# Pair sums and splits regrouped around the gating pair of a one-layer decoder block

## The chip, the core and the metric

The kernel runs on one core of a Trainium2 chip. The metric is the device time of one execution in microseconds. TensorE (PE in the profile) multiplies, VectorE (DVE) and ScalarE (ACT) do elementwise work, GpSimd (POOL) does little here, and SyncE (SP) issues nearly all loads.

## The reference

One layer over 256 tokens of width 2048, all in float32:

```python
h = rms_norm(x, norm_mix_pre)
proj = h @ w_in                                  # columns of A, B, C and the merge gates
y_a = conformer_conv(a_in, ...)                  # GLU, causal conv, layer norm, swish, projection
y_b = chunked_spatial_gating(b_in, ...)          # gelu, spatial mix by chunks, projection
y_c = native_sparse_attention(q, kv, nsa_g, ...) # three attention branches, projection
g_a, g_b, g_c = split(sigmoid(merge_g), 3)
mixed = (g_a * y_a + g_b * y_b + g_c * y_c) @ w_o
x = x + rms_norm(mixed, norm_mix_post)
h = rms_norm(x, norm_ffn_pre)
u = causal_depthwise_conv(h @ w_up, ...)
x = x + rms_norm((silu(u_g) * u_v) @ w_down, norm_ffn_post)
```

## The kernel before, in words

**Products of split numbers.** Every float32 matrix operand is split into a rounded high part and the rest: ScalarE copies the high part (`whi`, or `whiwraw` where it goes through `weights`), VectorE subtracts it from the raw weights (`wlo`, `wlowraw`). A product is three matmuls: high by high, high by low, low by high. Weights come as tiles of 128 x 1024 into `wraw`, a ring of five buffers; the high parts and the rests have a ring of four each. A load can start when its buffer's last reader is done, a split when TensorE has read the buffer it writes.

**Sevens.** Three products, the last gating pair (column blocks 2 and 3 of branch C's merge gates), the first half of `w_o` and both halves of `w_down`, run in a scheme of seven products for a 2 x 2 block of 128 x 512 tiles (`class Seven`). It needs sums of pairs of k-tiles, on the activations' side (`sums4`, `input_sums`) and on the weights' side (in `seven`, on VectorE and ScalarE: parts named b, a, t and 4). A call works through plain k-tiles of 12 matmuls each and quads of 21; `in_sevens` uses 10 plain k-tiles (k = 6 to 15) and 3 quads (k = 0 to 5). Four banks (`pga`, `poa`) hold the main results, four others (`pgb`, `pob`) the side results that `combine` adds up.

**The order of the work.** The stages are: input projections with the attention spread between them; `branch` for B, A and C, each of which multiplies gate columns (`pg`), takes the tanh of the gates (`mg`), multiplies a branch's projection (`py`) and adds the gated product into `mac`. Branch C is called for blocks 0 and 1 only. Then comes the gating pair (`in_sevens` into `pga` and `pgb`), its results `gates` (VectorE adds, ScalarE tanh), the projections of C for blocks 2 and 3 (`pyc`, `pyd`), the output pair (`po2`, in `poa` and `pob`), the rest of `w_o`, and the feed-forward part with `w_up` and `w_down` (`Pair(0)` in `pd0a` and `pd0b`, `Pair(1)` in `pd1a` and `pd1b`).

**Who decides the order.** Each engine works through its instructions in the order in which they stand. A scheduler sets that order by priority; `fixed` chains an instruction behind the last `fixed` one of its engine (`seq`), `order_of` sets where these chains begin, `in_line` chains matmuls, and `issue_after` puts one instruction behind another. Background generators (`bg`) are advanced by `pump` and `until`. `mix_gen(cb)` is one of them: for block `cb` it transposes `mac` on TensorE (`pm`), splits it into `mh` (ScalarE) and `ml` (VectorE), and for the first three pairs of k-tiles copies the transposed blocks (`ma`, ScalarE) and calls `sums4`, whose adds go to `spm` and `sqm` and whose results are split into `sm`. `sm` is read by the quads of the output pair.

**The last norm.** `fin` holds the down projection's result `res` (columns 0 to 4095), a row of weights `gain` (from 4096) and two scratch areas of 1536 columns for the quads (from 5120 and from 6656). `result` adds a bank to a part of `res` and sums its squares on ScalarE; `weigh` multiplies a part by `gain`, on VectorE. The first half's four parts are weighed during the second pass over `w_down`; then the other half of the row is loaded over `gain`.

Of the kernel before, what the change touches and what calls it, by code (L numbers as in the profile page):

```python
# [25 lines left out]
R = mybir.dt.float32r  # L26
AF = mybir.ActivationFunctionType
# [30 lines left out]
def block(ctx: ExitStack, tc: tile.TileContext, x, xf, fp, cst, rows, sgw, w1, w2, wf_a, wt_bv, wf_bu, wf_c,  # L58
# [197 lines left out]
    def s8(shape, dt, name):  # L256
        return P1.tile(shape, dt, tag="s8", bufs=4, name=name)
# [631 lines left out]
    def fixed(eng, op, *args, **kw):  # L889

        with ExitStack() as order:
            order.enter_context(tc.high_priority())
            for ins in seq.get(eng, ()):
                order.enter_context(tc.issue_after(ins))
            seq[eng] = [op(*args, **kw).ins]  # L895

    def order_of(last):
        seq[V] = seq[S] = list(last)
# [90 lines left out]
    mac = s16(P0, [128, 2, D], F32, "mac")  # L989
    mix = {}  # L990

    def branch(bi, act_of):

        for cb in range(2 if bi == 2 else 4):
            pg = [PS.tile([128, 512], F32, tag="acc", name=f"pg{bi}{cb}{t}") for t in range(2)]
            for q in range(4):
                hs = granule(wt_g[(bi * 4 + cb) * 4 + q])
                for k in range(4 * q, 4 * q + 4):
                    hi, lo = hs[(k % 4) // 2]
                    c = slice((k % 2) * 512, (k % 2) * 512 + 512)  # L1000
                    for t in range(2):
                        ts = slice(t * 128, t * 128 + 128)
                        mm_t(pg[t], hT[:, k, 0, ts], hT[:, k, 1, ts], hi[:, c], lo[:, c], k == 0, k == KT - 1)
                if q < 3:
                    pump(BUDGET)
            tgs = {}
            for t in range(2):
                for a in range(2):
                    tgs[t, a] = q1(f"mg{bi}{cb}{t}{a}")
                    with tc.high_priority(offset=int(PR)):  # L1010
                        S.activation(tgs[t, a], pg[t][:, a * 256:a * 256 + 256], AF.Tanh, scale=rh[:, t:t + 1])
            marks.add("gates")
            pump(BUDGET)
            py = [PS.tile([128, 512], F32, tag="acc", name=f"py{bi}{cb}{t}") for t in range(2)]
            for q in range(2):
                hs = granule(wt_p[(bi * 4 + cb) * 2 + q])
                if cb == 0 and q == 0:
                    until("BAC"[bi])
                    if bi == 2:
                        mix["h"] = s16(P1, [128, KT, T], R, "mh")  # L1020
                        mix["l"] = s16(P1, [128, KT, T], R, "ml")
                act = act_of()
                for k in range(4 * q, 4 * q + 4):
                    hi, lo = hs[(k % 4) // 2]
                    c = slice((k % 2) * 512, (k % 2) * 512 + 512)
                    for t in range(2):
                        ts = slice(t * 128, t * 128 + 128)
                        pe_last[0] = mm_t(py[t], act[:, k, 0, ts], act[:, k, 1, ts], hi[:, c], lo[:, c], k == 0, k == 7)
                if q == 0:
                    pump(BUDGET)  # L1030
            for t in range(2):
                for a in range(2):
                    cc = slice(cb * 512 + a * 256, cb * 512 + a * 256 + 256)
                    y = mac[:, t, cc] if bi == 0 else tgs[t, a]
                    with tc.high_priority(offset=int(PR)):
                        V.scalar_tensor_tensor(y, tgs[t, a], 1.0, py[t][:, a * 256:a * 256 + 256], op0=ALU.add,
                                               op1=ALU.mult)
                        if bi:
                            V.tensor_add(mac[:, t, cc], mac[:, t, cc], y)
            if bi == 2:  # L1040
                bg.append(mix_gen(cb))
            pump(BUDGET)

    def mix_gen(cb):

        for j in range(2 * cb, 2 * cb + 2):
            pt = bank([128, 2, T], f"pm{j}")
            ks = slice(2 * j, 2 * j + 2)
            for i in range(2):
                for t in range(2):  # L1050
                    PE.transpose(pt[:, i, t * 128:t * 128 + 128], mac[:, t, (2 * j + i) * 128:(2 * j + i) * 128 + 128],
                                 ident)
            S.activation(mix["h"][:, ks], pt, AF.Copy, scale=0.5)
            V.scalar_tensor_tensor(mix["l"][:, ks], pt, 0.5, mix["h"][:, ks].bitcast(F32), op0=ALU.mult,
                                   op1=ALU.subtract)
            yield 500
            if j < NG:
                a = [q1(f"ma{j}{i}") for i in range(2)]
                for i in range(2):
                    S.activation(a[i], pt[:, i], AF.Copy, scale=0.5)  # L1060
                if j % 2 == 0:
                    mix[j // 2] = s8([128, 2, 2, 4, 128], R, f"sm{j}")
                sums4(a[0], a[1], mix[j // 2][:, j % 2], f"m{j}")
                yield 1500

    branch(0, lambda: Bt_box["t"])
    branch(1, lambda: At)
# [17 lines left out]
    def acts_h(j):  # L1085
        s1, s2, s4, s3 = parts(sh[:, j], range(4))
        return s4, hx(2 * j + 1, H1), hx(2 * j, H1), s1, s3, s2, hx(2 * j + 1, H2)

    order_of(())
    in_sevens(pr, wt_gp, wt_gq, hx, acts_h, tt, "g")  # L1090
    for n in range(2):
        for t in range(2):
            fixed(V, V.tensor_add, gates[:, t, n], pr.c[t][n], gates[:, t, n])
            fixed(S, S.activation, gates[:, t, n], gates[:, t, n], AF.Tanh, scale=rh[:, t:t + 1])
    pump(1e6)
    Ct = Ct_box["t"]
    for n in range(2):
        cb = 2 + n
        py = [bank([128, 512], f"pyc{t}") if n == 0 else PS.tile([128, 512], F32, tag="acc", name=f"pyd{t}")
              for t in range(2)]  # L1100
        for k in range(8):
            if k % 2 == 0:
                hi, lo = weights(wt_p[(8 + cb) * 2 + k // 4][:, k % 4 * 512:k % 4 * 512 + 1024])
            c = slice(k % 2 * 512, k % 2 * 512 + 512)
            for t in range(2):
                ts = (H1, H2)[t]
                in_line(mm_t, py[t], Ct[:, k, 0, ts], Ct[:, k, 1, ts], hi[:, c], lo[:, c], k == 0, k == 7)
        for t in range(2):
            cc = slice(cb * 512, cb * 512 + 512)
            with tc.high_priority(offset=int(PR)):  # L1110
                V.scalar_tensor_tensor(gates[:, t, n], gates[:, t, n], 1.0, py[t], op0=ALU.add, op1=ALU.mult)
                V.tensor_add(mac[:, t, cc], mac[:, t, cc], gates[:, t, n])
        bg.append(mix_gen(cb))
        pump(1e6)
# [277 lines left out]
    P2c = ctx.enter_context(tc.tile_pool(name="p2c", bufs=1))  # L1392
    fin = P0.tile([128, 8192], F32, tag="hT", name="fin")
    res = fin[:, 0:4096].rearrange("p (t n) -> p t n", t=2)
    gain = fin[:, 4096:5120]
    turn = [0]

    def scratch():
        turn[0] ^= 1
        return fin[:, 5120 + 1536 * turn[0]:6656 + 1536 * turn[0]]  # L1400

    ss3 = PZ.tile([128, 2, 8], F32, name="ss3")
    G.memset(ss3, 0.0)
    nc.sync.dma_start(gain, row(2048, 1024))


    order_of(())
# [1 line left out]
    class Pair(Seven):  # L1409
# [40 lines left out]
                                   accum_out=ss3[:, t, col + 1:col + 2])  # L1450

        def weigh(self, t, n, do=loose):
            do(V, V.tensor_mul, self.at(t, n), self.at(t, n), gain[:, n * 512:n * 512 + 512])

    NP, NQ, KEEP = len(PLAIN), len(PAIRS), 6

# [14 lines left out]
    for j in range(NQ):  # L1471
        while i < (3, 5, 7, 9, 10, 12, 14, 15, 17, 18)[j]:
            second.plain(i)
            if i == 2:
                for t in range(2):
                    for n in range(2):
                        first.result(t, n, fixed)
            elif 3 <= i < 7:
                first.weigh((i - 3) // 2, (i - 3) % 2, fixed)
            elif i == 9:  # L1480
                nc.sync.dma_start(gain, row(3072, 1024))
            i += 1
        second.quad(j)
        if j == 5:
            back = s16(P0, [128, 2, D], F32, "back")
            for t in range(2):
                nc.sync.dma_start(back[:, t], spill[:, t])
        for x in range(0 if j < NQ - 5 else 1 if j < NQ - 1 else KEEP - 4):
            k = NP - KEEP + len(kept)
            into = None  # L1490
            if j < NQ - 1:
                kt = P2.tile([128, 11, T], R, tag=("gh", "gl")[j % 2], bufs=4, name=f"kept{k}")
                into = kt[:, 0:8].rearrange("p (a b) c -> p a (b c)", a=2)
            kept.append((PLAIN[k], weights(wt_dn[1, k], into)))
    assert i == NP - KEEP and len(kept) == KEEP
    second.combine()
    for t in range(2):
        for n in range(2):
            c = slice(n * 512, n * 512 + 512)
# [141 lines left out]
```

## Time and profile before

| | us |
|---|---|
| median of 3 runs | 1584.13 |
| lowest and highest run | 1583.61, 1585.96 |
| profiled execution | 1585.73 |
| its span | 1584.0 |
| mean granted clock of TensorE | 0.996 of full |
| TensorE busy | 1565.5 |
| VectorE busy | 1275.7 |
| ScalarE busy | 907.1 |
| loaded from memory | 301.23 MB, 193 GB/s over the span |

Lines such as `687.65 0.39 PE L198 MATMUL py<-whi,Ct 128*128 128x512 f32 x1` are rows of the timeline: start in us from the span's start, duration, engine, source line, operation, what is written and what is read, shape, how many. Matmuls overlap, so their pace is read from start to start and not from the duration. A bracket at the end gives the idle time of the engine before the row and the instruction that ended it. In the list of waits a row reads: engine, what it wants to do and its line, who released it, us in total, how often, the longest.

### The profile page before, as it was taken

The page shows a single profiled execution, that of the slowest core. Times are in us where ns is not written, and L with a number is a line of the kernel's source. Part 1 is how long each engine was busy: PE and PEld are TensorE (multiplying, and loading weights), DVE is VectorE, ACT ScalarE, POOL GpSimd, SP SyncE. Part 2 cuts the span into 40 slices and gives each one's busy share as a digit, 9 for nine tenths or more (in the row PEclk, how much of TensorE's full clock was granted, in tenths as well). Part 3 has the DMA queues.
Part 4 walks back from the last instruction along what each step waited for, and adds up shares of the span by engine and source line. Part 5 has one row for each costly group of instructions (what it writes and reads, how often), then busy time and mean ns, then how long its engine had stood idle before and what let it go on. Part 6 is the DMA issues. An engine that isn't in the chain of part 4 may idle for free.

```text
span 1584.0 us, 22431 instructions
## 1 busy us (share of the span) xinstructions
PE 1565.5 (99%) x8155; PEld 1326.1 (84%) x8155; DVE 1275.7 (81%) x2192; ACT 907.1 (57%) x1462; POOL 17.8 (1%) x46
## 2 busy tenths in 40 slices
PE   9999999999999999999999999999999999999997
PEld 7888899888888787777888888888888888888876
DVE  7899999867866655477787988888777777899997
ACT  7544544447637675655465656565555555556563
POOL 1000020000000000000000000000000000000000
PEclk9999999999999999999999999999999999999999
DMA  9555566666765544445784666666656666766672
GB/s 375 186 190 184 187 179 208 195 187 186 243 194 155 160 146 153 139 160 188 245 273 145 210 192 188 193 188 189 187 188 192 191 190 190 232 205 209 213 268 78
DMA packets 85440, 307.95 MB, mean 194 GB/s; under 512 B 9808, under 2 KB 10832, under 8 KB 84304
## 3 DMA queue, kind: packets, MB, share of 16 engines
q1 hardware_dynamic: 83952, 301.91, 60.0%
q0 software_dynamic: 944, 4.19, 0.7%
q8 instruction: 64, 1.05, 0.3%
q10 hardware_dynamic: 432, 0.41, 0.1%
q14 instruction: 48, 0.39, 0.1%
HBM read 301.23 MB, written 4.19 MB: 193 GB/s over the span
## 4 chain that ended last, share of the span: by engine, by line
PE 50%; DVE 2%; DMA 1%; issue 0%; ACT 0%; DVEq 0%; ACTq 0%
PE ps L176 20%; PE ps L183 10%; PE pd0b L930 5%; PE pd1a L930 4%; PE poa L930 2%; PE pd0a L930 2%; PE po L196 1%; PE po L198 1%; PE po L197 1%; PE pd1b L930 1%; DMA wraw<-in_wt_dn_dram 1%; PE pob L930 1%; DVE wlowraw L895 0%; DVE fin L895 0%; PE pu L1239 0%
## 5 line engine op out<-in xcount | busy, mean ns | idle before, releaser
L148 DVE TENSOR_TENSOR wlo<-wraw,whi 128x1024 fp32r<-128x1024 f32 x400 | 486.7, 1219 | 116.0 <-ACT whi L147 109.5
L147 ACT ACTIVATE whi<-wraw 128x1024 fp32r<-128x1024 f32 x400 | 419.0, 1053 | 187.3 <-PE pg L198 78.4
L176 PE MATMUL ps<-h2T,whi 128*128 128x512 f32 x1360 | 325.0, 391 | 0.0
L176 PEld LDWEIGHTS ps<-h2T,whi 128*128 128x128 f32 x1360 | 249.8, 188 | 48.2
L183 PEld LDWEIGHTS ps<-h2T,wlo 128*128 128x128 f32 x1360 | 174.5, 191 | 6.7
L183 PE MATMUL ps<-h2T,wlo 128*128 128x256 f32 x1360 | 176.6, 283 | 0.0
L176 PE MATMUL ps<-hT,whi 128*128 128x512 f32 x640 | 157.4, 392 | 0.0
L218 ACT ACTIVATE t<-ps 128x256 f32<-128x256 f32 x125 | 47.6, 382 | 187.1 <-PE ps L176 186.6
L176 PEld LDWEIGHTS ps<-hT,whi 128*128 128x128 f32 x640 | 116.0, 188 | 21.3
L198 PE MATMUL pg<-whi,hT 128*128 128x512 f32 x320 | 125.8, 393 | 0.0
L197 PE MATMUL pg<-wlo,hT 128*128 128x512 f32 x320 | 125.8, 393 | 0.0
L196 PE MATMUL pg<-whi,hT 128*128 128x512 f32 x320 | 122.2, 393 | 0.0
L895 DVE TENSOR_TENSOR wlowraw<-wraw,whiwraw 128x1024 fp32r<-128x1024 f32 x72 | 87.0, 1224 | 33.6 <-ACT whiwraw L895 32.5
L219 DVE TENSOR_TENSOR t<-ps,t 128x256 f32<-128x256 f32 x125 | 52.7, 422 | 70.3 <-ACT t L218 69.8
L479 DVE SCALAR_TENSOR_TENSOR cv<-hb,fps,cv 128x256 f32<-128x256 f32 x240 | 105.0, 478 | 0.2 <-ACT cv L475 0.2
L895 ACT ACTIVATE whiwraw<-wraw 128x1024 fp32r<-128x1024 f32 x72 | 75.4, 1056 | 43.6 <-PE pyc L198 9.0
L183 PEld LDWEIGHTS ps<-hT,wlo 128*128 128x128 f32 x640 | 84.7, 190 | 4.7
L183 PE MATMUL ps<-hT,wlo 128*128 128x256 f32 x640 | 86.8, 283 | 0.0
L197 PEld LDWEIGHTS pg<-wlo,hT 128*128 128x128 f32 x320 | 60.1, 188 | 13.7 <-issue 1.1
L198 PEld LDWEIGHTS pg<-whi,hT 128*128 128x128 f32 x320 | 60.1, 188 | 12.7 <-issue 0.7
L196 PEld LDWEIGHTS pg<-whi,hT 128*128 128x128 f32 x320 | 59.8, 188 | 12.4 <-issue 0.3
L1372 ACT ACTIVATE fa<-fs,fps 128x256 f32<-128x256 f32 x88 | 52.5, 597 | 1.2 <-DVE fs L221 0.9
(1258 smaller groups left out, 2659.3 us busy)
## 6 DMA issues: line engine op xcount, KB each, us to landing
wraw<-in_wf_up_dram SPq DMA_DIRECT2D x176, 512.0 KB, 4.3
wraw<-in_wt_g_dram SPq DMA_DIRECT2D x80, 512.0 KB, 4.1
wraw<-in_wt_p_dram SPq DMA_DIRECT2D x48, 512.0 KB, 4.2
wraw<-in_wt_dn_dram SPq DMA_DIRECT2D x48, 512.0 KB, 4.5
wraw<-in_wf_a_dram SPq DMA_DIRECT2D x32, 512.0 KB, 4.1
wraw<-in_wt_dq_dram SPq DMA_DIRECT2D x20, 512.0 KB, 4.8
qa<-in_wt_dq_dram SPq DMA_DIRECT2D x20, 512.0 KB, 4.2
wraw<-in_wf_bu_dram SPq DMA_DIRECT2D x16, 512.0 KB, 4.4
```

The costliest lines, as they stand in the source:

```text
L147: S.activation(hi[:, :n], raw[:, :n], AF.Copy)
L148: V.tensor_sub(lo[:, :n], raw[:, :n], hi[:, :n].bitcast(F32))
L176: ins = PE.matmul(ps[:, :, ts], lhsT=ws[k // 8][0][:, c:c + 128], rhs=mov[:, k, :, ts], start=(k == 0 and not t), stop=(k == n - 1), skip_ ...
L183: ins = PE.matmul(ps[:, 1, ts], lhsT=ws[k // 8][1][:, c:c + 128], rhs=mov[:, k, 0, ts], start=False, stop=False, skip_group_check=True).ins
L196: PE.matmul(ps, lhsT=xh, rhs=hi, start=first, stop=False)
L197: PE.matmul(ps, lhsT=xh, rhs=lo, start=False, stop=False)
L198: return PE.matmul(ps, lhsT=xl, rhs=hi, start=False, stop=last).ins
L219: V.tensor_add(t1 if rb is not None else dst, ps[:, 0], t1)
L479: V.scalar_tensor_tensor(ca[:, j], hb[:, j, k:k + T], w(j, k), ca[:, j], op0=ALU.mult, op1=ALU.add)
L895: seq[eng] = [op(*args, **kw).ins]
L930: ins = PE.matmul(bank, lhsT=a[x], rhs=w[y], start=first and j == 0, stop=last and j == 2).ins
L1372: S.activation(a, s, AF.Identity, bias=fps[:, C_FB + f:C_FB + f + 1], scale=w[2])
```

## The change

It has three parts.

1. `mix_gen` no longer calls `sums4`; it leaves its `ma` copies in `mix["a", j]`. The three calls stand behind the last of the gating pair's result adds (`issue_after(seq[V][0])`). All background work that is left is pumped before the gating pair instead of after it, and ScalarE's chain of the gating pair begins behind the last tanh of branch C's gates (`gated`).
2. The splits for three of the eight weight tiles of `pyc` and `pyd` are put into the two engines' chains ahead of the gating pair's results: two ahead of all of them, the third ahead of those of block 3.
3. `gain` is widened to 2048 columns, so that its second half lies on the scratch area that the last quad uses. The load of the second half stands behind the last load of weights, and the four `weigh` calls of the first half stand behind `second.combine()`.

In the order of the instructions this moves the following. On ScalarE, the first four splits of the gating pair go behind `mh`, the four `ma` copies and the four tanh `mg`; two more `ma` copies go behind quad 0's splits. On VectorE, 12 adds (`spm`, `sqm`) and 6 rests of `sm` leave the first part of the gating pair and stand behind its results, among the rests of `pyc`'s and `pyd`'s weights. On TensorE, the eight transposes of block 1 stay among the same k-tiles but no longer in one group; those of block 2 go from the middle of `pyd` to its end and behind the sixth `poa` matmul; those of block 3 go from inside k-tile 8's matmuls to around the last matmuls of k-tile 7. The loads of weights keep their order.

```diff
@@ branch
-                        S.activation(tgs[t, a], pg[t][:, a * 256:a * 256 + 256], AF.Tanh, scale=rh[:, t:t + 1])
+                        gated[0] = S.activation(tgs[t, a], pg[t][:, a * 256:a * 256 + 256], AF.Tanh,
+                                                scale=rh[:, t:t + 1]).ins
@@ mix_gen
-                if j % 2 == 0:
-                    mix[j // 2] = s8([128, 2, 2, 4, 128], R, f"sm{j}")
-                sums4(a[0], a[1], mix[j // 2][:, j % 2], f"m{j}")
-                yield 1500
+                mix["a", j] = a
@@ the gating pair
+    def wp(n, k):
+        return weights(wt_p[20 + 2 * n + k // 4][:, k % 4 * 512:k % 4 * 512 + 1024])
+
+    pump(1e6)
     order_of(())
+    seq[S] = [gated[0]]
     in_sevens(pr, wt_gp, wt_gq, hx, acts_h, tt, "g")
+    early = [wp(0, k) for k in (0, 2)]
     for n in range(2):
         for t in range(2):
             fixed(V, V.tensor_add, gates[:, t, n], pr.c[t][n], gates[:, t, n])
             fixed(S, S.activation, gates[:, t, n], gates[:, t, n], AF.Tanh, scale=rh[:, t:t + 1])
+        if n == 0:
+            early.append(wp(0, 4))
+    with tc.issue_after(seq[V][0]):
+        for j in range(NG):
+            if j % 2 == 0:
+                mix[j // 2] = s8([128, 2, 2, 4, 128], R, f"sm{j}")
+            sums4(*mix["a", j], mix[j // 2][:, j % 2], f"m{j}")
@@ pyc and pyd
-                hi, lo = weights(wt_p[(8 + cb) * 2 + k // 4][:, k % 4 * 512:k % 4 * 512 + 1024])
+                hi, lo = early.pop(0) if early else wp(n, k)
@@ the last norm
-    gain = fin[:, 4096:5120]
+    gain = fin[:, 4096:6144]
-    nc.sync.dma_start(gain, row(2048, 1024))
+    nc.sync.dma_start(gain[:, 0:1024], row(2048, 1024))
-            do(V, V.tensor_mul, self.at(t, n), self.at(t, n), gain[:, n * 512:n * 512 + 512])
+            x = self.p * 1024 + n * 512
+            do(V, V.tensor_mul, self.at(t, n), self.at(t, n), gain[:, x:x + 512])
-            elif 3 <= i < 7:
-                first.weigh((i - 3) // 2, (i - 3) % 2, fixed)
-            elif i == 9:
-                nc.sync.dma_start(gain, row(3072, 1024))
+    nc.sync.dma_start(gain[:, 1024:2048], row(3072, 1024))
     second.combine()
+    for t in range(2):
+        for n in range(2):
+            first.weigh(t, n, fixed)
```

More of the change, by code (lines that the diff above doesn't have):

```diff
@@ L990, in block @@
     mix = {}
+    gated = [None]
     def branch(bi, act_of):
```

## The prediction

> **What bounds the kernel now.** The page's engine shares come first, then TensorE's waits, which say what is left to win.
>
> ```profile
> PE 1565.5 (99%) x8155; PEld 1326.1 (84%) x8155; DVE 1275.7 (81%) x2192; ACT 907.1 (57%) x1462; POOL 17.8 (1%) x46
> ...
> PE pga L930 <- ACT mg L1011: 2.5, 1, 2.5
> PE pyc L196 <- ACT whiwraw L895: 2.5, 1, 2.5
> ...
> PE pd1a L930 <- DVE wlowraw L895: 1.2, 2, 0.6
> PE pyc L197 <- DVE wlowraw L895: 0.7, 1, 0.7
> ...
> PE pga L930 <- DVE wlog0b L895: 0.2, 1, 0.2
> ```
>
> TensorE works through 99% of the span, so nothing is gained by making another engine's work cheaper: time moves only where TensorE stands, where its clock is low, and behind its last matmul. Four of these five waits (5.9 us) lie in the gating pair, which the change rearranges. The two waits of pd1a belong to the down projection.
>
> The windows view says that the idle time is not the whole price. Its columns are the stretch, its length, the busy time of PE, PEld, DVE, ACT and POOL, the granted clock, the DMA share and GB/s.
>
> ```profile
> 688.10:690.50 2.40, 0.00 (x0) 0.00 (x0) 1.91 (x5) 2.10 (x5) 0.00 (x0) 1.00 0.74 207
> ...
> 734.60:737.00 2.40, 0.00 (x0) 0.00 (x0) 0.70 (x2) 2.40 (x5) 0.00 (x0) 1.00 0.00 0
> ...
> 739.00:744.00 5.00, 5.00 (x13) 3.87 (x12) 2.66 (x3) 1.43 (x2) 0.00 (x0) 0.50 0.81 243
> ```
>
> After the second gap the granted clock is 0.50 for 5 us and more, in which TensorE counts as busy; after the first it stays 1.00. The timeline of TensorE measures both:
>
> ```profile
> 687.65 0.39 PE L198 MATMUL py<-whi,Ct 128*128 128x512 f32 x1
> 690.54 0.50 PE L930 MATMUL pga<-whiwraw,hT 128*128 128x512 f32 x1 [2.50 <-ACT mg L1011]
> ...
> 696.20 1.03 PE L1051 MATMUL pm<-idn,mac 128*128 128x128 f32 x8
> 696.99 0.48 PE L930 MATMUL pga<-whiwraw,hT 128*128 128x512 f32 x1
> ...
> 726.25 0.39 PE L930 MATMUL pga<-whiwraw,hT 128*128 128x512 f32 x1
> ...
> 734.18 0.39 PE L930 MATMUL pga<-whiwraw,hT 128*128 128x512 f32 x1
> 737.05 0.55 PE L196 MATMUL pyc<-whiwraw,Ct 128*128 128x512 f32 x1 [2.49 <-ACT whiwraw L895]
> 738.31 0.80 PE L197 MATMUL pyc<-wlowraw,Ct 128*128 128x512 f32 x1 [0.71 <-DVE wlowraw L895]
> ...
> 744.34 0.39 PE L196 MATMUL pyc<-whiwraw,Ct 128*128 128x512 f32 x1
> ```
>
> From 726.25 to 734.18 are 35 matmuls start to start, 0.2266 us each: the undisturbed pace. The gating pair is 183 matmuls (10 k-tiles of 12, 3 quads of 21). From the last py to the last pga, 46.53 us hold 183 paces (41.47) and 8 transposes (696.99 - 696.20 = 0.79): **4.27 us are lost**, 2.66 at the first gap and the rest mostly at quad 0, whose rests come a little late from VectorE. From 734.18 to 744.34, 10.16 us hold 16 paces (3.63): **6.53 us are lost**, of which 3.20 is idle and 3.3 is half clock and restart. Together 10.8 us, 0.7% of the run: the most that the first two parts can bring.
>
> **The change part by part.** *Splits of the gating pair behind the gates' tanh.* The first gap ends when ScalarE has read pg's bank. Its queue shows why so late:
>
> ```profile
> 681.78 1.07 ACT L1053 ACTIVATE mh<-pm 128x512 fp32r<-128x512 f32 x2
> ...
> 683.82 0.64 ACT L1060 ACTIVATE ma<-pm 128x256 f32<-128x256 f32 x2
> ...
> 689.67 1.55 ACT L1011 ACTIVATE mg<-pg,rh 128x256 f32<-128x256 f32 x4
> ```
> ```profile
> 681.91 1.23 DVE L895 TENSOR_TENSOR wlowraw<-wraw,whiwraw 128x1024 fp32r<-128x1024 f32 x1 [3.08 <-ACT whiwraw L895]
> 683.05 1.28 DVE L1054 SCALAR_TENSOR_TENSOR ml<-pm,mh 128x512 fp32r<-128x512 f32 x2
> 685.38 0.29 DVE L840 TENSOR_TENSOR spm<-ma,ma 128x128 f32<-128x128 f32 x1
> ...
> 687.64 0.42 DVE L847 TENSOR_TENSOR sm<-spm,sm 128x256 fp32r<-128x256 f32 x1
> ...
> 691.17 1.41 DVE L1036 SCALAR_TENSOR_TENSOR mg<-mg,py 128x256 f32<-128x256 f32 x4
> ```
>
> Four splits, four ma copies and four sm copies stand around the tanh, and copies and splits wait for VectorE and back. In the new order ScalarE does mh, ma and mg without a split between them: mh still starts at 681.78 (its transposes do not move), ma ends about 684.4 (two pairs of 0.64, behind the ml), mg at 684.4 + 1.55 = 685.95, before py's last matmul (688.04). So the bank wait goes. Next late is the first split itself: hi at 685.95 + 1.06 = 687.0, its rest (1.23) at 688.2, needed at 688.1: no wait to speak of. Behind it on VectorE stand two gate products (0.7) and the second rest, done about 690.05; TensorE wants that at 687.88 + 7 x 0.2266 = 689.5. I charge 0.5 us for this new wait with its restart; the ends are 0 (rests back to back) and 2.66 (the gap stays whole, only caused by the splits). The nearest rows, the durations above, say near the low end.
>
> *Pair sums moved behind the results.* The issue list of the loads gives a landing time, its last column:
>
> ```profile
> wraw<-in_wt_oq_dram SPq DMA_DIRECT2D x6, 512.0 KB, 4.8
> ```
>
> Three sums of four adds (0.2 start to start), two sm copies and two sm rests (0.42) leave VectorE before quad 0: about 1.5 us each, 4.5 in all. Quad 0's first difference then starts about 694.3, directly behind the last mac sum (from 690.05: two more rests and four sums of 0.34 start to start), and its second half has landed by then: its buffer is freed by the first rest at 688.2, 4.8 before 693.0. Its three rests follow by 696.9, 698.6 and 700.3 at VectorE's pace. TensorE wants them at 688.3 + 48 x 0.2266 + 0.8 = 700.0, 701.4 and 702.7. So quad 0's lateness (1.6 of the 4.27) goes. The mix's transposes of block 1 stay among the same k-tiles, and the bank that quad 0's last products take is free about 701.6, for 702.7: 1.1 us in hand. Where the sums go, VectorE has room: they run in the pyc stage, and their readers are the output pair's quads, 144 matmuls (33 us) behind pyc's first. **Part one: 4.27 - 0.5 = 3.8 us.**
>
> *Output weights split ahead of the results.*
>
> ```profile
> 726.73 0.58 ACT L895 ACTIVATE gates<-pgb 128x512 f32<-128x512 f32 x1
> 733.29 2.76 ACT L895 ACTIVATE gates<-gates,rh 128x512 f32<-128x512 f32 x4 [5.98 <-DVE gates L895]
> 735.96 3.88 ACT L895 ACTIVATE whiwraw<-wraw 128x1024 fp32r<-128x1024 f32 x4
> ```
> ```profile
> 728.00 2.73 DVE L895 TENSOR_TENSOR gates<-pgb,gates 128x512 f32<-128x512 f32 x4
> 732.57 2.73 DVE L895 TENSOR_TENSOR gates<-pga,gates 128x512 f32<-128x512 f32 x4 [1.83 <-PE pga L930]
> ```
>
> ScalarE idles 5.98 us, then does four tanh that wait for pga's last matmul, and only then the split that pyc waits for. Now two splits stand before the tanh. All times 3.8 earlier: pga ends about 730.6. Split 1 goes at 723.5 (behind the pgb copy), its rest on VectorE behind the four pgb adds, done 727.8 for 730.6. Split 2 waits for a buffer that TensorE frees at 725.2; rest 729.0 for 733.3. Split 3 stands behind two tanh: rest 733.3 for 736.1. Split 4 behind the other two, its rest behind ten short sums: 737.8 for 738.8, the narrowest. The loads are two buffers ahead. So neither the 3.20 of idle nor the half clock behind it is left: **6.5 us**, with 6.53 as the upper end and, as the lower, 3.2 if the half clock came without a gap.
>
> [...]
>
> *Transposes of blocks 2 and 3, moved with mac.* Block 2's eight transposes go from the middle of pyd to between pyd and the sixth output matmul; they cost the same there. Their products are read first by k-tile 8, 24 matmuls and 16 transposes (some 7 us) behind. ScalarE and VectorE need about 5 for copy, rest and what stands in front. No cost; the cover is 2 us.
>
> *Last norm.* Four products and a load leave the middle of the second down pass for its end.
>
> ```profile
> 1480.36 0.69 DVE L895 TENSOR_TENSOR fin<-fin 128x512 f32<-128x512 f32 x1
> ...
> 1521.26 1.23 DVE L895 TENSOR_TENSOR wlowraw<-wraw,whiwraw 128x1024 fp32r<-128x1024 f32 x1 [2.43 <-ACT whiwraw L895]
> ...
> 1559.11 2.73 DVE L895 TENSOR_TENSOR fin<-pd1b,fin 128x512 f32<-128x512 f32 x4
> 1562.56 0.69 DVE L1348 TENSOR_TENSOR fin<-pd1a,fin 128x512 f32<-128x512 f32 x1 [0.72 <-PE pd1a L930]
> ```
> ```profile
> 1564.03 1.28 ACT L1503 ACT_TABLE_LOAD   x1
> ...
> 1567.37 0.63 ACT L1348 ACTIVATE junk<-fin 128x512 bf16<-128x512 f32 x1 [1.61 <-DVE fin L1348]
> ```
> ```profile
> fin<-in_rows_dram SPq DMA_DIRECT2D x2, 512.0 KB, 5.1
> ```
> ```profile
> 1557.74 17.04 PE pd1a L930 x75
> ```
>
> Taken away there: 4 x 0.6 of VectorE about 1480. The two pd1a waits (1.2) come some 50 us later, behind a stretch in which VectorE idles for a late split (2.43 before 1521.26), so a lead does not reach them: gain 0; the upper end is their 1.2. Put in at the end: 2.4 us from 1561.8, so the first result goes from 1562.56 to 1564.2. ScalarE's square, table load and warm-up then end about 1567.36, against 1567.37 for the next square. Loss 0, up to 0.4 if each step is a little longer. The load waits for the last quad's scratch, free two rests (2 x 1.2) before 1559.11, so about 1556.7; it lands 5.1 later at 1561.8 and is read at about 1565.6; behind it on SP's queue are only the output stores. Cost 0.
>
> Sum: 3.8 + 6.5 - 0.1 = 10.2 us. The profiled execution is 1585.73 with a span of 1584.0: it becomes 1575.5 (span 1573.8). The median of the three runs, 1584.13, lies 1.6 below that execution; taken off it, 1573.9. I take **1574.5**, between.
>
> **The rivals.** *The half clock is shorter in the median run* (0.15). The half-clock stretch costs 3.3 here; were the 1.6 us between this execution and the median a shorter stretch, the median would win only 8.6: 1575.5. For it: the runs spread by 2.4 us; against: nothing shows the clock of those runs. [...]
>
> *One gap survives in a new form* (0.15). If the splits behind mg arrive 2.2 us later than worked out, the first gap keeps its 2.66: 1576.7. If split 4's rest misses its 1.0 us of cover by a further 1 us and the clock halves behind it, 4.3 come back: 1578.8. Against both: each duration is read from a row, and the order is fixed.
>
> *Slower* (0.05). At the start of the output pair VectorE must take quad 0's first difference before block 2's rests (ml), and that waits for a load of 512 KB, 4.8 by its row, requested about 748 and wanted at 756. TensorE wants the rests at 759.8. [...] From a landing time of 8 us it costs anything; to pass before's time it must eat 10.2, so 7 of stall and 3.3 of clock, a landing time of about 18: at 20, 1586. The profile has 14.1 for one broadcast load, nothing like it for weights.
>
> **How the numbers follow.** The forecast has 0.65 and stands for 1572.5 to 1575.5; the others as given. The low end is both parts in full with the smaller clock cost, 1584.13 - 10.8 - 1.2 (the pd1a waits too), about 1572; the high end takes in a surviving gap, 1578.8. A measurement tells 0.2% (3.2 us) from no change. Faster by more than that: all cases but slower and a combination of the two middle ones with a lost tail, 0.91; same 0.04; slower 0.05.
>
> **What would show it.** TensorE's list of waits without mg and without whiwraw before pyc; a granted clock of 1.00 throughout 730 to 745; at most 0.5 us of wait on wlowraw at the first k-tiles; pyc's first matmul near 730.6; no wait in poa; pd1a's two waits as before; 9.2 us from the end of the last matmul (1557.74 + 17.04 = 1574.8) to the end of the span, as before. It is wrong if the half clock shows up elsewhere, if poa waits for ml, or if the tail grows by more than 0.5.

## The result, and the profile after

| | before | after |
|---|---|---|
| median of 5 runs, us | 1584.65 | 1574.49 |
| lowest and highest run | 1583.61, 1585.96 | 1572.95, 1575.5 |
| profiled execution (span) | 1585.73 (1584.0) | 1575.5 (1573.8) |
| mean granted clock | 0.996 | 0.998 |

The ratio is 0.9934, with an interval of 0.9919 to 0.9948: 10.2 us faster, 0.66%. On another chip the same kernel took 1573.03 against 1585.29, ratio 0.9927 (0.9915 to 0.9939).

The page of the changed kernel opens with these lines; the list of TensorE's waits, which follows, is complete (what TensorE wants, who released it, us in total, how often, the longest).

```profile
span 1573.8 us, 22431 instructions
...
PE 1561.2 (99%) x8155; PEld 1324.4 (84%) x8155; DVE 1274.0 (81%) x2192; ACT 906.6 (58%) x1462; POOL 17.7 (1%) x46
```
```profile
PE warm L288 <- POOL wz L285: 1.4, 1, 1.4
PE pd1a L930 <- DVE wlowraw L895: 1.2, 2, 0.6
PE pv L402 <- ACT swraw L118: 0.3, 1, 0.3
```

All four waits in and behind the gating pair are gone; the two of pd1a stand as before. The windows view (stretch, length, busy time of PE, PEld, DVE, ACT, POOL, then the granted clock, the DMA share and GB/s) shows the stretches that held the two gaps and the half clock:

```profile
688.20:690.50 2.30, 2.20 (x10) 1.56 (x9) 2.30 (x5) 1.54 (x2) 0.00 (x0) 1.00 0.51 125
...
730.00:735.00 5.00, 5.00 (x24) 4.14 (x23) 3.24 (x5) 2.74 (x4) 0.00 (x0) 1.00 0.57 203
735.00:740.00 5.00, 5.00 (x24) 4.14 (x23) 4.93 (x15) 5.00 (x10) 0.00 (x0) 1.00 0.44 125
```

TensorE's timeline measures what is left:

```profile
687.94 0.39 PE L198 MATMUL py<-whi,Ct 128*128 128x512 f32 x1
688.16 0.39 PE L930 MATMUL pga<-whiwraw,hT 128*128 128x512 f32 x1
...
689.30 0.61 PE L930 MATMUL pga<-whiwraw,hT 128*128 128x512 f32 x2
690.01 0.50 PE L930 MATMUL pga<-wlowraw,hT 128*128 128x512 f32 x1
...
730.90 0.39 PE L930 MATMUL pga<-whiwraw,hT 128*128 128x512 f32 x1
731.13 0.39 PE L196 MATMUL pyc<-whiwraw,Ct 128*128 128x512 f32 x1
...
734.53 0.39 PE L196 MATMUL pyc<-whiwraw,Ct 128*128 128x512 f32 x1
```

From the last py to the last pga are 42.96 us; 183 paces of 0.2266 and eight transposes (0.79) make 42.26. **0.70 is lost where 4.27 was**: 0.26 at 689.30 (two matmuls take 0.71 instead of 0.45), 0.11 right behind it, the rest in small steps around transposes that no longer stand in one group. From 730.90 to 734.53 are 16 paces (3.63): **nothing is lost where 6.53 was.** Behind the last matmul the end has its old length: 1573.8 - (1564.18 + 0.39) = 9.2.

The rest of the difference between the two profiles is chance. This execution reaches the gating pair 0.29 later than the one before did, and loses 0.37 less in the second down pass: 3.57 + 6.53 + 0.37 - 0.29 = 10.2, the difference of the spans.

### The profile page after: what moved, and what is told of

The parts are those of the page before. It is cut to its first block, busy times and chain, and to the rows that moved or that the text cites. A ratio compares the mean times of both kernels' runs of the same rounds, so it can differ in the third digit from the quotient of the medians.

```text
span 1573.8 us, 22431 instructions
## 1 busy us (share of the span) xinstructions
PE 1561.2 (99%) x8155; PEld 1324.4 (84%) x8155; DVE 1274.0 (81%) x2192; ACT 906.6 (58%) x1462; POOL 17.7 (1%) x46
## 4 chain that ended last, share of the span: by engine, by line
PE 96%; DVE 2%; DMA 1%; ACT 0%; issue 0%; DVEq 0%; SPq 0%; ACTq 0%
PE ps L176 29%; PE ps L183 15%; PE pd0b L930 5%; PE pg L197 5%; PE pg L198 5%; PE pg L196 5%; PE pd1a L930 4%; PE py L197 2%; PE py L198 2%; PE py L196 2%; PE poa L930 2%; PE pga L930 2%; PE pd0a L930 2%; PE po L198 1%; PE po L196 1%; PE po L197 1%
```

## The experiments

Two stretches are compared below. One goes from the last py to the last poa, that is, over the gating pair, pyc, pyd and the output pair; the same matmuls and transposes lie in it in every kernel. It takes 118.53 us before and 108.43 in the changed kernel, 10.10 less, which is 3.57 + 6.53. The other is the second down pass: from its first matmul to its last, less 497 paces, 3.6 us are lost before and 3.2 in the changed kernel.

### The output splits not put ahead

```diff
-    early = [wp(0, k) for k in (0, 2)]
+    early = []
...
-        if n == 0:
-            early.append(wp(0, 4))
```

> The changed kernel without its second part: no output weights are split ahead of the gating pair's results. Theory (each gap has its own cause): the first gap stays away and quad 0 is in time, so the stretch from the last py to the last pga keeps its 3.8 us of gain; the gap ahead of pyc comes back with 2.5 us for the split and 0.7 to 1.7 for its rest, which now stands behind the moved sums. What follows it tells two theories of the half clock apart. If an idle time of this length always halves the clock, the granted clock falls to 0.50 for some 6 us behind it and the time is 6.5 to 7.5 above the changed kernel, about 1581.5. If it is a matter of phase, the clock may stay at 1.00 and the time is 3.2 to 4.2 above it, about 1578.

Measured: median 1579.8, ratio 0.9974 (0.9964 to 0.9983). Its TensorE stands again in front of pyc, and its clock is halved behind that (timeline, then windows of this kernel):

```profile
730.41 0.39 PE L930 MATMUL pga<-whiwraw,hT 128*128 128x512 f32 x1
733.29 0.49 PE L196 MATMUL pyc<-whiwraw,Ct 128*128 128x512 f32 x1 [2.49 <-ACT whiwraw L895]
734.99 0.80 PE L197 MATMUL pyc<-wlowraw,Ct 128*128 128x512 f32 x1 [1.20 <-DVE wlowraw L895]
```
```profile
734.40:734.60 0.20, 0.00 (x0) 0.00 (x0) 0.20 (x1) 0.20 (x1) 0.00 (x0) 0.90 0.00 0
737.80:738.00 0.20, 0.20 (x2) 0.20 (x1) 0.20 (x1) 0.20 (x1) 0.00 (x0) 0.57 0.57 184
```

From the last py to the last poa it takes 114.11 us, 5.7 more than the changed kernel; the ratios, 0.9974 against 0.9934, put the difference at 6.3. So the second part of the change is worth about what the prediction gave it (6.5), although in this profile it is made up otherwise: more idle time (3.7) and a shorter half clock. The clock falls at 734.56 (0.90 over 0.2 us leaves 0.04 at half) and rises at 737.97: 3.41 us, where the profile of before has 6.82.

### The pair sums left where they were

```diff
-                mix["a", j] = a
+                if j % 2 == 0:
+                    mix[j // 2] = s8([128, 2, 2, 4, 128], R, f"sm{j}")
+                sums4(a[0], a[1], mix[j // 2][:, j % 2], f"m{j}")
+                yield 1500
```

> The changed kernel with the pair sums left where the background generator emits them, ahead of quad 0; the splits still stand behind the tanh, the early output splits stay. Theory (the sums on VectorE and their copies on ScalarE are what held the tanh back and made quad 0 late): the tanh ends about 687.8, the first k-tile waits 1 to 2 us for its split and rest, quad 0's rests are late again by about 1 us; together 2 to 3.5 us above the changed kernel. Rival (the splits ahead of the tanh were the cause): the same time as the changed kernel within 0.5.

Measured: median 1576.97, ratio 0.9957 (0.9941 to 0.9974). From the last py to the last poa it takes 110.56 us, 2.1 more than the changed kernel, and all of that lies in the gating pair, where 2.81 is lost instead of 0.70. From its list of waits:

```profile
PE pm L1054 <- DVE mac L1042: 0.9, 2, 0.6
PE pd1a L930 <- DVE wlowraw L895: 0.9, 2, 0.6
PE pga L930 <- DVE wlowraw L895: 0.6, 1, 0.6
```

The wait for the bank (mg) does not return, since the tanh stand ahead of the splits, but VectorE is late with everything behind: the rests, and the mac sums that the transposes read.

### The splits free to go ahead of the tanh

```diff
-    seq[S] = [gated[0]]
```

> The changed kernel with ScalarE's chain of the gating pair free again: two splits stand ahead of the tanh, as in the kernel before, the sums stay moved. Theory (sums as the cause): the tanh ends about 688, as py's last matmul starts, so at most 0.3 us of wait for the bank, and the first two rests are earlier, which takes away the 0.3 us of lateness at the first k-tiles: the same time as the changed kernel within 0.4. Rival (the splits ahead of the tanh were the cause): the first gap is back with 1.5 to 2.5 us.

Measured: median 1572.61, ratio 0.9931 (0.9916 to 0.9946). No wait of pga is left, and the 0.26 and 0.11 of the changed kernel are gone too: from the last py to the last pga 0.29 us is lost, where that kernel loses 0.70 (0.72 in a second profile). ScalarE does two splits ahead of the tanh and still ends the tanh at 685.86, in time for pga (ScalarE, then TensorE):

```profile
680.20 1.06 ACT L895 ACTIVATE whiwraw<-wraw 128x1024 fp32r<-128x1024 f32 x1 [3.25 <-PE py L198]
681.16 1.07 ACT L1056 ACTIVATE mh<-pm 128x512 fp32r<-128x512 f32 x2
682.23 1.06 ACT L895 ACTIVATE whiwraw<-wraw 128x1024 fp32r<-128x1024 f32 x1
...
684.29 1.57 ACT L1013 ACTIVATE mg<-pg,rh 128x256 f32<-128x256 f32 x4
```
```profile
687.03 0.39 PE L198 MATMUL py<-whi,Ct 128*128 128x512 f32 x1
687.26 0.39 PE L930 MATMUL pga<-whiwraw,hT 128*128 128x512 f32 x1
```

The gating pair loses 4.27 with neither piece of part one, 2.81 with the splits behind the tanh alone, 0.29 with the moved sums alone and 0.70 with both. So it is the moved sums that clear the first gap. The line that puts the splits behind the tanh is not needed once they are moved, and costs 0.4. In the last three of these the background work is also pumped ahead of the pair; what that does by itself was not run.

### The last norm alone, and the rest alone

The third part was put into the kernel before, and taken out of the changed one (its three pieces in the diff, applied and reverted).

```diff
-    gain = fin[:, 4096:5120]
+    gain = fin[:, 4096:6144]
...
+    for t in range(2):
+        for n in range(2):
+            first.weigh(t, n, fixed)
```

> The kernel before with the last norm's part alone. Theory: the same time as before within 0.4 us, both gaps and the half clock of before in place. It also is a second look at the half clock of the old order: if the length of the half-clock stretch is a matter of phase, it may be shorter or missing here, with the 3.2 us of idle unchanged; if an idle time of this length always brings it, it lasts some 6 us again.

> The changed kernel with the last norm as before: the four products and the load back in the middle of the second down pass. Theory: no difference to the changed kernel, 0 +- 0.3 us in the span; pd1a's two waits (1.2 us) stay. Rival: the freed VectorE time in the middle was worth something, and this kernel is 0.6 to 1.2 us slower with longer pd1a waits.

Measured: alone 1583.64, ratio 0.9998 (0.9988 to 1.0007); the change without it 1573.49, ratio 0.9936 (0.9921 to 0.995), against the whole change's 0.9934. Neither shows a gain or a loss; the intervals leave room for some 1.5 us. The profile without it had a span of 1571.0, 2.8 shorter than the changed kernel's: 0.8 of that came ahead of the gating pair and 2.0 in the second down pass (1.2 lost against 3.2). The experiments on the reload ask whether that was the edit.

### Four more products at the end

Two kernels weigh the first half twice, so that eight products stand at the end; their output is changed by it. The first only adds them, and the second also holds the second half's results behind them.

```diff
             first.weigh(t, n, fixed)
+            first.weigh(t, n, fixed)
```
```diff
-                second.result(t, n, loose)
+                with tc.issue_after(seq[V][0]):
+                    second.result(t, n, loose)
```

> The changed kernel with the first half weighed twice behind the last quad, eight products for four (this half of the down projection's result is multiplied by its weights twice, which changes the output). Theory (the four products are hidden, with less than 0.5 us in hand): the second four push the first result from 1554.0 to 1556.4, the square, table load and second square behind it by as much, and with VectorE in one chain to the end the span grows by 1.7 to 2.4 us. Rival (VectorE has slack there): the span grows by less than 0.5.

> The changed kernel with the first half of the residual's result weighed twice, so that eight products instead of four stand in a row on VectorE ahead of the first result of the second half; its output is changed by that. The prediction took four products of 0.6 us as just fitting ahead of the point from which the end would grow. If that is right, the first result goes from about 1554.0 to about 1556.4 and the square, the table load and the second square behind it go along: span 1.7 to 2.4 us longer, the end of the last matmul unchanged. If there is more room than worked out, the span grows by less than 0.5.

Measured: 1573.72 (ratio 0.9935, 0.992 to 0.995) and 1575.38 (0.9938, 0.9923 to 0.9953). In the first the time did not grow, since the scheduler put the first result ahead of most products and spread these over idle time of VectorE, so it tested something else than meant. In the second they stand in a row (its VectorE):

```profile
1550.76 5.39 DVE L895 TENSOR_TENSOR fin<-fin 128x512 f32<-128x512 f32 x8
1556.06 1.28 DVE L1361 TENSOR_TENSOR fin<-pd1a,fin 128x512 f32<-128x512 f32 x2
...
1568.28 2.87 DVE L1534 SCALAR_TENSOR_TENSOR fin<-fin,rsyd,back 128x512 f32<-128x512 f32 x5
```

The last matmul starts at 1563.33 here and at 1564.18 in the changed kernel; against it the first result comes 2.9 later, the second square 2.6 later, the last products and the end 1.55 later (tail 10.8 against 9.2). The forecast of 1.7 to 2.4 was a little high: 1.3 us of the delay found room. So the four products of the change fit, with about that much to spare.

### The residual's reload

The second down pass reloads the residual (`back`, two loads of 1 MB) in the middle of its weights. In one kernel's source it comes in four pieces behind quads 5 to 8, in another's behind the last weights; the edit of the first is

```diff
-            for t in range(2):
-                nc.sync.dma_start(back[:, t], spill[:, t])
+        if 5 <= j < 9:
+            t, c = (j - 5) // 2, slice(j % 2 * 1024, j % 2 * 1024 + 1024)
+            nc.sync.dma_start(back[:, t, c], spill[:, t, c])
```

> The changed kernel with the reload of the residual (two loads of 1 MB in a row, ahead of the weights of the second down pass) cut into four of 0.5 MB, one behind each of four quads' loads. Theory (these two loads hold back the next weights, 10 us to landing, VectorE idles 2.4 us for them and is late by that until the end of the pass): the late split goes, pd1a's two waits (1.2 us) and the lateness of some rests (together 2.5 us) with it, and the time is 1.5 to 2.8 us below the changed kernel. Rival (VectorE alone is the bound of this stretch): no gain, within 0.4.

> The changed kernel with the reload of the residual behind the last load of weights. Theory as for the spread reload: 1.5 to 2.8 us below the changed kernel, as the weights no longer wait for 2 MB; the reload is issued about 1536 and has landed by 1550, before the residual is added at 1559.6. Rival: the reload lands late or delays the weights' row of the last norm behind it, and the tail grows by 1 us or more.

Measured: 1573.0 (ratio 0.9929, 0.9914 to 0.9944) and 1573.91 (0.9934, 0.9919 to 0.9949); the second down pass loses 1.2 and 2.0 us. The forecast of 1.5 to 2.8 us below the changed kernel (0.9934) did not come. The trace shows that the loads were not where the source has them. These are the reload's issues in the changed kernel, with the four pieces and in the late place (duration in ns, then first and last start):

```profile
L1499 SPq DMA_DIRECT2D back<-spill x2: 327/376/424, 1498.8 to 1499.2; - x2
L1500 SPq DMA_DIRECT2D back<-spill x4: 326/453/1392, 1498.6 to 1501.8; - x4
L1507 SPq DMA_DIRECT2D back<-spill x2: 326/374/422, 1498.4 to 1499.2; - x2
```

The scheduler put them forward. The four pieces go out within 3.2 us with two loads of weights between them, and the reload that was to leave about 1536 leaves at 1498.4, with one load of weights between its halves. So neither kernel tested a later reload; they tested the same place with loads of weights between. Then the changed kernel was profiled once more, beside a kernel with the four pieces and without the splits' place behind the tanh:

> The changed kernel as it is, a second look on the chip of the other three. Its gating pair should again lose less than 0.5 us and keep the clock at 1.00 from 730 to 745. In the down pass: if the late split behind the reload is a matter of load, it need not come back (pd1a waits 0.5 or 1.2 us, span 1570.5 to 1574); if it belongs to the place of the reload, pd1a waits 1.2 again and the span is 1573.5 or more.

> The changed kernel, with ScalarE's chain of the gating pair free to begin ahead of the last tanh and the residual reloaded in four pieces behind the second down pass's quads. If the two experiments before it measured separate things, both add: no lateness at the gating pair's first k-tiles (0.3 to 0.4 us less) and, in the down pass, one wait of pd1a of about 0.5 in place of 1.2 with some 2 us less lost there (the reload's landing decides). Span 1570.5 to 1572, median 1571.5 to 1573.5, ratio 0.9915 to 0.993. If the landing of the reload varies by run and not by its place, the median lies within 0.5 of that of the changed kernel on the same chip.

Measured: the changed kernel 1573.03 (1572.81 to 1574.41), span 1571.3, the gating pair as in its first profile (0.72 lost), the clock full, one wait of pd1a of 0.5, and 1.2 lost in the second down pass instead of 3.2. Nothing was edited; only the load came sooner. The loads' median time from issue to landing, and ScalarE's splits, in the first profile of the changed kernel:

```profile
back<-spill SPq DMA_DIRECT2D x2, 1024.0 KB, 8.4
```
```profile
1506.51 1.04 ACT L895 ACTIVATE whiwraw<-wraw 128x1024 fp32r<-128x1024 f32 x1
1510.03 1.06 ACT L895 ACTIVATE whiwraw<-wraw 128x1024 fp32r<-128x1024 f32 x1 [2.48 <-DMA wraw<-in_wt_dn_dram]
```

and in its second:

```profile
back<-spill SPq DMA_DIRECT2D x2, 1024.0 KB, 6.2
```
```profile
1506.04 1.05 ACT L895 ACTIVATE whiwraw<-wraw 128x1024 fp32r<-128x1024 f32 x1
1507.33 1.06 ACT L895 ACTIVATE whiwraw<-wraw 128x1024 fp32r<-128x1024 f32 x1 [0.24 <-DMA wraw<-in_wt_dn_dram]
```

In the eleven profiles with the reload in its old place, the loss of the second down pass goes with its landing time: 8.3 to 8.7 us lose 3.2 to 3.6 (five), 7.3 to 7.5 lose 2.2 to 2.4 (three), 6.1 to 6.3 lose about 1.2 (three). So the shorter span without the last norm needs no edit to explain it. Why the landing time differs is open, and so is whether the reload holds the weights back or something else delays both.

The combined kernel took 1572.56 (1572.23 to 1572.72), ratio 0.9922 (0.991 to 0.9934), span 1570.5. It has the lowest median of all, 0.5 us below the changed kernel on the same chip, of which its gating pair explains 0.4 (0.29 lost): its five runs lie below that one's five, but the intervals of the ratios overlap, and the gain expected from the reload was not there in the profile, since in the changed kernel's second profile the reload landed early as well. What the pieces may bring is steadiness: with them the runs span 0.5 and 0.8 us, in the changed kernel 1.6 and 2.6, but these are four or five runs each.

### The kernel before, a second time

> The kernel before as it is, a second profile. The two gaps (2.5 at pga behind mg; 2.5 with 0.5 to 0.7 at pyc) are set by the order of the instructions and should be there again to within 0.1. The half clock behind them should not be the same if it is a matter of phase: behind each gap none, about 3.4 us or about 6.7 us. If it is a matter of the gap's length alone, it is again 1.00 behind the first and 0.50 for some 6.6 us behind the second.

Measured: 1584.4, span 1582.7. The two gaps are the same (its timeline):

```profile
690.47 0.50 PE L930 MATMUL pga<-whiwraw,hT 128*128 128x512 f32 x1 [2.50 <-ACT mg L1011]
...
736.95 0.51 PE L196 MATMUL pyc<-whiwraw,Ct 128*128 128x512 f32 x1 [2.48 <-ACT whiwraw L895]
738.21 0.80 PE L197 MATMUL pyc<-wlowraw,Ct 128*128 128x512 f32 x1 [0.75 <-DVE wlowraw L895]
```

and so is the clock: full behind the first gap, half for 6.8 us behind the second. The 1.3 us by which this span is shorter lie in the second down pass (2.2 lost against 3.6; the reload landed in 7.4 instead of 8.7). But in the kernel with the last norm alone, whose instructions up to there are those of before, the same first gap of 2.50 did halve the clock, for 3.41 us. So the gap's length alone does not decide it; what does is not shown.

## Why the prediction was right

**The sum.** 1574.5 was forecast, 1574.49 and 1573.03 are the medians; 10.2 us of span were forecast and came. Two terms carry it: 3.57 against 3.8 in the gating pair and 6.53 against 6.5 at the output projections. The 0.1 that the sum takes off has no term of its own.

**Splits behind the tanh.** The queue ran as it was worked out (ScalarE, then VectorE, changed kernel):

```profile
684.38 1.57 ACT L1013 ACTIVATE mg<-pg,rh 128x256 f32<-128x256 f32 x4
685.81 3.93 ACT L895 ACTIVATE whiwraw<-wraw 128x1024 fp32r<-128x1024 f32 x4
```
```profile
686.93 1.23 DVE L895 TENSOR_TENSOR wlowraw<-wraw,whiwraw 128x1024 fp32r<-128x1024 f32 x1 [3.13 <-ACT whiwraw L895]
...
688.74 1.22 DVE L895 TENSOR_TENSOR wlowraw<-wraw,whiwraw 128x1024 fp32r<-128x1024 f32 x1
...
694.15 0.68 DVE L895 TENSOR_TENSOR tt<-wraw,wraw 128x512 f32<-128x512 f32 x1
```

mg ends at 685.95 as forecast, the first rest at 688.16 (688.2), the second at 689.96 (690.05), and the lateness behind it is 0.37, charged at 0.5. (These are times of two executions, and this one has py's last matmul 0.29 later; counted from there, each step came 0.3 to 0.4 early.) What was wrong is whom the step credits: the place of the splits was given the bank wait, and the run without it shows that the wait is gone with the moved sums alone, and that this place costs 0.4 of the 0.70 that is left.

**Sums moved.** Quad 0's first difference was forecast for 694.3 and starts at 694.15; its lateness is gone. Leaving the sums in place costs 2.1 of the 3.57. In their new place no wait of poa names them.

**Output splits ahead.** Right in size and in both halves: without them idle and half clock return, 5.7 together in that profile. The fourth rest was called the narrowest, done 737.8 for 738.8. It starts at 737.29, ends at 738.5, and TensorE wants it 37 paces behind 731.13, at 739.5: the same 1.0 of cover.

**Transposes and late loads.** No wait at the output pair: the 0.05 rival of a late load there found nothing.

**Last norm.** In before's times the first result was put at 1564.2 and the square at 1567.37; less 10.2 that is 1554.0 and 1557.17.

```profile
1551.62 2.48 DVE L895 TENSOR_TENSOR fin<-fin 128x512 f32<-128x512 f32 x4
1554.02 0.68 DVE L1361 TENSOR_TENSOR fin<-pd1a,fin 128x512 f32<-128x512 f32 x1
```
```profile
1557.17 0.63 ACT L1361 ACTIVATE junk<-fin 128x512 bf16<-128x512 f32 x1
```

The tail kept its 9.2. That pd1a's waits would stay was right for this execution, and the reason (a late split that no lead reaches) too, but they are no fixed term: they went with the reload's landing, 0.5 in one profile and 1.2 in another. The prediction carried them as constant; the forecast's accuracy to a hundredth is therefore luck, and about 2 us, by which the second down pass differs between profiles of one kernel, is the fair measure of it.

**The rivals.** The half clock does differ between runs, as that rival held: in 35 runs of the kernel before, the mean granted clock was 0.996 or above in 24, 0.995 in nine and 0.994 in two; the means of the groups with 0.996, 0.995 and 0.994 are 1583.89, 1585.75 and 1587.12 us. A thousandth of the clock over 1584 us at half speed costs 1.6 by arithmetic, and the groups stand 1.9 and 1.4 apart. For the 1.6 us between the first profile of before and its median the reload is the likelier cause: that profile has 0.996, as the group whose mean lies 1.8 lower, and its reload landed last of all (8.7). The two gaps in a new form did not come. The slower rival's prices do not add up: lateness from a landing time of 8 and 7 us of stall make a landing time of 15, not 18, and at 20 the time would be 1574.5 + 12 + 3.3 = 1589.8, not 1586. Nor does any run show that a stall of a given length brings the 3.3 of clock in its sum: the first gap of 2.50 left the clock at 1.00 in both profiles of before and halved it for 3.41 us in the kernel with the last norm alone.

## What to carry to other kernels

An engine at 99% can still have its time in two short gaps: measure the matmuls against their own pace over the stretch, since the half clock behind a gap counts as busy (before, TensorE was busy for all 5.00 us from 739 to 744, at a granted clock of 0.50) and appears in no list of waits. Where an engine waits in a ring (ScalarE on VectorE on ScalarE), look for the work in the ring that nobody needs soon; here 12 small adds with six rests opened it, and with them gone the order of the urgent work was worth 0.4. Before a difference of 2 us between two profiles is given to an edit, profile the same kernel twice. Where a scheduler sets the order, read in the trace when a moved load really leaves: three of the edits here (the first with four more products, and both of the reload) did not run as their source reads.

## What the runs showed of the hardware

**The half clock came in stretches of 3.41 or 6.82 us.** In the kernel with the last norm alone the clock falls and rises twice; windows of 0.2 us place the edges (a mean of 0.81 over 0.2 us leaves 0.076 at half, so the fall is at 690.12).

```profile
690.00:690.20 0.20, 0.00 (x0) 0.00 (x0) 0.20 (x1) 0.20 (x2) 0.00 (x0) 0.81 0.99 410
693.40:693.60 0.20, 0.20 (x2) 0.20 (x1) 0.20 (x1) 0.00 (x0) 0.00 (x0) 0.66 0.67 266
737.80:738.00 0.20, 0.00 (x0) 0.00 (x0) 0.00 (x0) 0.20 (x1) 0.00 (x0) 0.78 0.00 0
744.60:744.80 0.20, 0.20 (x2) 0.20 (x1) 0.00 (x0) 0.03 (x1) 0.00 (x0) 0.66 0.87 266
```

Half clock from 690.12 to 693.54 and from 737.91 to 744.74: 3.41 and 6.82 us, and the two falls are 47.79 apart, 14.0 times 3.41. In the kernel before the second gap's half clock goes from 737.37 to 744.20, again 6.82:

```profile
737.20:737.40 0.20, 0.20 (x1) 0.04 (x1) 0.20 (x1) 0.20 (x1) 0.00 (x0) 0.93 0.00 0
744.00:744.20 0.20, 0.20 (x2) 0.17 (x1) 0.00 (x0) 0.20 (x1) 0.00 (x0) 0.51 0.66 225
```

In the second profile of before it lasts 6.8 again, and without the output splits put ahead 3.41.

The length of the gap alone does not tell whether the clock falls. The first gap was 2.50 in both profiles of before and in the kernel with the last norm alone. In the first two the clock stayed at 1.00 behind it; in the third it fell 1.97 us into the gap (TensorE's last matmul ends at 688.15). In the 3.41 us that end with each of the other four falls TensorE idled 1.99 to 2.92; since the ends of matmuls are modelled in the profile, these figures could be a little larger. In the first 3.41 us at half clock it idled 0.43 and 0.53 in the two cases where the clock then rose, and 0.68, 0.71 and 0.96 in the three where it stayed at half for as long again. What decides between these cases is not shown.

**One transfer's landing time differs by 2.6 us from run to run, and the loss behind it goes along.** The same two loads of 1 MB in the same place of the queue landed in 6.1 to 8.7 us, and TensorE lost 1.2 to 3.6 us in that pass; in four pieces of 0.5 MB with weights between them, 1.2 was lost in both profiles, with median landing times of 6.1 and 7.7. That it is the reload which holds the weights back is not shown.
